# Four edits at the head of a decoder layer's first projection: who asks for the loads, who casts, in what pieces

## The chip, the cores and the metric

The kernel runs on one core of a Trainium2 chip. A core has five engines with instruction rows of their own: TensorE (PE in the profile; PEld is its weight load), VectorE (DVE), ScalarE (ACT), GpSimd (POOL) and SyncE (SP). Any of SP, ScalarE and GpSimd can ask for a load; 16 DMA engines then move it. An engine works its row in order and waits where a semaphore is not there yet. The metric is device time in microseconds, the median over several executions of the same program; one execution is profiled.

## The reference

One layer of a decoder over 272 rows (16 meta tokens and 256 of input) of width 2048. Only the first projection is touched by the change; the rest is given in outline.

```python
u = rmsnorm(h, norm_mix)
proj = u @ w_in            # 2048 x 7176: q, k, v, gates of 8 retention and 4 mLSTM heads
...
ret = head_norm(retention_chunkwise(...)) * silu(g_r)
hm = head_norm(mlstm_chunkwise(...)) * sigmoid(o_m)
h = h + concatenate([ret, hm]) @ w_out
u = rmsnorm(h, norm_ffn)
up = causal_dwconv(u @ w_up, ffn_conv_w, ffn_conv_b)
gate, val = split(up)
h = h + (silu(gate) * val) @ w_down
out = rmsnorm(h, norm_final)[N_META:]
```

## The kernel before

**Number format.** Every product is made in three matmuls. A float32 operand is split into a high part (a cast to float32r) and a low part (the rest), and high x high, high x low and low x high are summed in PSUM. For weights, the cast is on ScalarE (`whi`) and the subtraction on VectorE (`wlo`); for the activations likewise (`xh` on ScalarE, scaled by the norm's weight; `xl` on VectorE). The scale by the row's root mean square comes after the product, so no matmul has to wait for the norm.

**The ramp** (lines 206 to 238) is the start of the program. The contraction over 2048 is cut into 16 k tiles of 128. The loop takes k = 0 and k = 1 alone and then seven pairs. For each step it loads `hT` (the transposed input, 272 columns for a k tile) and `wraw` (320 columns of weights for a k tile: 128 for a key, 128 for a query, 64 for the gates, from `in_w0`), makes `xh`, `xl`, `whi`, `wlo`, and a low part of the gate weights (line 227, written behind the high part in `whi`), and issues eight matmuls for a k tile: three for the key (`k_ps`), three for the query (`q_ps`), two for the gates (`gates_ps`, lines 235, 236 and 238). Lines 130, 131 and 133 are the three matmuls of the helper `mmk`. `par` holds all small parameters; its first 16 columns are the norm's weights, which every `xh` and `xl` reads.

**Who asks for the loads.** The weights of k = 0 and of k = 1 are asked for by ScalarE, all else by SP, in the order of the loop. `wraw` has four buffers, so the fifth load waits until VectorE is done with the first. The first `xT` load, `par`'s first columns and the rest of the `xT` loads stand on SP one behind another.

**Warm-up.** Before the loop TensorE runs `WARM` matmuls of `ones` with itself, whose result is not used; they start when VectorE has set `ones` (line 171), its third memset.

**Behind the ramp** come 108 loads of 512 KB for the rest of the projection (`load_w`: cast on ScalarE, line 121; low part on VectorE, line 123), the first of them for `v0_ps`, the sum of squares for the norm (line 252 squares, line 255 adds), and then the heads, the output projection, the up-projection and the down-projection, all in the same style. A scheduler sets the final order of each engine's row from the order and the priorities in the code.

Of the kernel before, what the change touches and what calls it, by code (L numbers as in the profile page):

```python
# [10 lines left out]
F32 = mybir.dt.float32  # L11
F32R = mybir.dt.float32r
AF = mybir.ActivationFunctionType
ALU = mybir.AluOpType
PSUM = bass.MemoryType.PSUM

P = 128
# [14 lines left out]
HALF = KT // 2  # L32
GW = 64
W0 = GW + 2 * P
WARM = 8

# [45 lines left out]
def trunk(ctx: ExitStack, tc: tile.TileContext, io, out: bass.AP):  # L84
# [19 lines left out]
        return par[:, a + i : a + i + n]  # L104

    inv_dm = consts.tile([P, P], F32, name="inv_dm")
    nc.vector.memset(inv_dm, 1.0 / DM)
    epsc = consts.tile([P, 1], F32, name="epsc")
    nc.vector.memset(epsc, EPS)
    rstd2 = consts.tile([P, NQ], F32, name="rstd2")  # L110


# [56 lines left out]
    ident = pa.tile([P, P], F32, name="ident")  # L169
    ones = pa.tile([P, P], F32, name="ones")  # L170
    nc.vector.memset(ones, 1.0)
    inv_ret = pa.tile([P, P], F32R, name="inv_ret")
    inv_ml = pa.tile([P, P], F32R, name="inv_ml")
    rstd1 = pa.tile([P, T], F32, name="rstd1")
# [10 lines left out]
    kpad = [pa.tile([P, 3 * P], F32, name=f"kpad{i}") for i in range(2)]  # L185
    vpad = pa.tile([P, 3, 2 * P], F32, name="vpad")
    ppad = pa.tile([P, ABC], F32, name="ppad")
    for kt in kpad:
        nc.gpsimd.memset(kt[:, T:], 0.0)
    nc.gpsimd.memset(vpad[:, 2, :], 0.0)  # L190
# [15 lines left out]
    with pool("sq", 1, side="right") as sqp:  # L206
        for k0, k1 in [(0, 1), (1, 2)] + [(k, k + 2) for k in range(2, KT, 2)]:
            n = k1 - k0
            nc.sync.dma_start(hT[:, k0:k1, :], io["xT"][:, k0:k1, :])
            if k0 == 0:  # L210
                nc.sync.dma_start(par[:, 0:KT], io["par"][:, 0:KT])
            raw = wpool.tile([P, 2, W0], F32, name="wraw", bufs=4)[:, :n, :]

            queue = nc.scalar if k0 < 2 else nc.sync
            load = queue.dma_start(raw, io["w0"][:, k0:k1, :])
            if k0 >= 2:
                last_load = load
            for k in range(k0, k1):
                nc.scalar.activation(xh[:, k, :], hT[:, k, :], AF.Copy, scale=pcol("gmix", k))
                nc.vector.scalar_tensor_tensor(out=xl[:, k, :], in0=hT[:, k, :], scalar=pcol("gmix", k),  # L220
                                               in1=xh[:, k, :].bitcast(F32), op0=ALU.mult, op1=ALU.subtract)

            hi = wpool.tile([P, 2, W0 + GW], F32R, name="whi", bufs=5)[:, :n, :]
            copied = nc.scalar.copy(hi[:, :, 0:W0], raw)
            lo = wpool.tile([P, 2, 2 * P], F32R, name="wlo", bufs=5)[:, :n, :]
            nc.vector.tensor_tensor(out=lo, in0=raw[:, :, 0 : 2 * P], in1=hi[:, :, 0 : 2 * P].bitcast(F32), op=ALU.subtract)
            parted = nc.vector.tensor_tensor(out=hi[:, :, W0:], in0=raw[:, :, 2 * P :], in1=hi[:, :, 2 * P : W0].bitcast(F32), op=ALU.subtract)
            for k in range(k0, k1):
                i = k - k0
                first, last = k == 0, k == KT - 1  # L230
                for j, (ps, t0) in enumerate(((k_ps, 0), (q_ps, TQ))):
                    w = hi[:, :, j * P : (j + 1) * P], lo[:, :, j * P : (j + 1) * P]
                    mmk(ps[:, : T - t0], w, [(i, k)], lambda k: xh[:, k, t0:], lambda k: xl[:, k, t0:], 0, KT - 1)
                if not last:
                    nc.tensor.matmul(gates_ps[:, :T], hi[:, i, 2 * P :], xh[:, k, :], start=first, stop=False)
                nc.tensor.matmul(gates_ps[0:GW, :T], hi[:, i, 2 * P : W0], xl[:, k, :], start=False, stop=False)
                if last:
                    nc.tensor.matmul(gates_ps[:, :T], hi[:, i, 2 * P :], xh[:, k, :], start=False, stop=True)
# [830 lines left out]
```

## Time and profile before

| what | us |
|---|---|
| runs shown | 1208.54, 1208.73, 1211.33 |
| their median | 1208.73 |
| the profiled execution | 1207.7 |
| its span, first to last instruction | 1205.9 |
| TensorE busy in the span | 1194.6 |
| ScalarE, VectorE, GpSimd busy | 709.5, 971.5, 162.8 |

The span is shorter than the execution's own time by what lies around the program's instructions (1.8 us). Busy time of TensorE counts matmuls with their modelled ends, so matmuls that follow one another overlap in it. Times in the timeline are counted from the start of the span.

### The profile page before, as it was taken

How to read it: one execution, taken by the hardware profiler on the slowest of the kernel's cores; microseconds unless marked ns; L12 is line 12 of the kernel's file. 1: busy time of each engine (PE TensorE's matmuls, PEld its weight loads, DVE VectorE, ACT ScalarE, POOL GpSimd, SP SyncE). 2: the span in 40 equal slices, each digit the busy share in tenths (PEclk: the TensorE clock that was granted, in tenths of full speed). 3: DMA queues.
4: the chain of work that ended last, by engine and by line, in shares of the span. 5: the costliest groups of instructions: out<-in, count | busy, mean ns of one | idle time of the engine just before them, and what ended most of it. 6: DMA issues, size and time to landing. Idle time of an engine off the chain costs nothing.

```text
span 1205.9 us, 22794 instructions
## 1 busy us (share of the span) xinstructions
PE 1194.6 (99%) x8956; PEld 1151.2 (95%) x8956; DVE 971.5 (81%) x1444; ACT 709.5 (59%) x963; POOL 162.8 (14%) x223
## 2 busy tenths in 40 slices
PE   9999999999999999999999999999999999999997
PEld 9999999999999999999999998878999999998886
DVE  8968788766775966789889879897788778789897
ACT  8747656655656646555555557664555555556664
POOL 0100001111110311021122100202022112100232
PEclk9999999999999999999999999999999999999999
DMA  8765555666565965766766834959787777755956
GB/s 278 269 212 164 170 184 170 197 183 192 169 192 165 349 200 175 252 220 212 253 219 214 279 117 175 278 177 276 284 251 255 223 240 249 261 176 211 274 181 186
DMA packets 83004, 263.27 MB, mean 218 GB/s; under 512 B 14672, under 2 KB 18896, under 8 KB 82768
## 3 DMA queue, kind: packets, MB, share of 16 engines
q1 hardware_dynamic: 71952, 223.85, 57.0%
q0 software_dynamic: 10368, 37.11, 10.1%
q8 instruction: 70, 1.15, 0.4%
q10 hardware_dynamic: 576, 0.85, 0.2%
q14 instruction: 38, 0.31, 0.1%
HBM read 243.42 MB, written 11.27 MB: 211 GB/s over the span
## 4 chain that ended last, share of the span: by engine, by line
PE 96%; DMA 2%; DVE 1%; ACT 0%; issue 0%; SPq 0%; DVEq 0%; ACTq 0%
PE mmps L130 26%; PE mmps L131 25%; PE mmps L133 25%; PE atps L827 2%; PE atps L828 2%; PE atps L830 2%; PE mmps L860 2%; PE mmps L862 2%; PE mmps L859 2%; PE atps L862 1%; PE atps L860 1%; PE atps L859 1%; DMA hn<-x 1%; PE atps L379 1%; DMA hT<-in_wd 1%; PE atps L371 0%
## 5 line engine op out<-in xcount | busy, mean ns | idle before, releaser
L121 ACT CAST whi<-wraw 128x1024 fp32r<-128x1024 f32 x352 | 369.3, 1050 | 342.0 <-PE mmps L131 228.7
L123 DVE TENSOR_TENSOR wlo<-wraw,whi 128x1024 fp32r<-128x1024 f32 x352 | 432.3, 1230 | 72.5 <-ACT whi L121 70.0
L130 PE MATMUL mmps<-uh,whi 128*128 128x258 f32 x1408 | 346.1, 283 | 0.0
L131 PE MATMUL mmps<-ul,whi 128*128 128x258 f32 x1408 | 346.0, 283 | 0.0
L130 PEld LDWEIGHTS mmps<-uh,whi 128*128 128x128 f32 x1408 | 267.6, 190 | 0.1
L131 PEld LDWEIGHTS mmps<-ul,whi 128*128 128x128 f32 x1408 | 267.1, 190 | 0.1
L130 PE MATMUL mmps<-xh,whi 128*128 128x272 f32 (+2 forms) x864 | 219.8, 288 | 0.0
L131 PE MATMUL mmps<-xl,whi 128*128 128x272 f32 (+2 forms) x864 | 218.3, 286 | 0.0
L133 PE MATMUL mmps<-uh,wlo 128*128 128x258 f32 x1408 | 196.5, 282 | 0.0
L133 PEld LDWEIGHTS mmps<-uh,wlo 128*128 128x128 f32 x1408 | 179.9, 189 | 0.0
L131 PEld LDWEIGHTS mmps<-xl,whi 128*128 128x128 f32 x864 | 162.8, 188 | 0.0
L130 PEld LDWEIGHTS mmps<-xh,whi 128*128 128x128 f32 x864 | 162.5, 188 | 0.1
L133 PE MATMUL mmps<-xh,wlo 128*128 128x272 f32 (+2 forms) x864 | 126.7, 285 | 0.0
L133 PEld LDWEIGHTS mmps<-xh,wlo 128*128 128x128 f32 x864 | 114.2, 188 | 0.0
L680 DVE TENSOR_TENSOR cu<-mmps,rstd 128x258 f32<-128x258 f32 x88 | 37.4, 425 | 55.3 <-PE mmps L133 54.8
L764 ACT CAST whi<-hT 128x1024 fp32r<-128x1024 f32 x52 | 53.6, 1052 | 27.2 <-PE atps L828 7.3
L766 DVE TENSOR_TENSOR wlo<-hT,whi 128x1024 fp32r<-128x1024 f32 x52 | 62.1, 1220 | 4.9 <-ACT whi L764 3.7
L131 PE MATMUL mmps<-mixl,whi 128*128 128x258 f32 x256 | 63.0, 283 | 0.0
L130 PE MATMUL mmps<-mixh,whi 128*128 128x258 f32 x256 | 62.4, 282 | 0.0
L764 ACT CAST whi<-wraw 128x1024 fp32r<-128x1024 f32 (+1 forms) x52 | 43.0, 838 | 16.8 <-PE mmps L860 6.8
L766 DVE TENSOR_TENSOR wlo<-wraw,whi 128x1024 fp32r<-128x1024 f32 (+1 forms) x52 | 52.2, 1037 | 0.6 <-PE mmps L862 0.2
L827 PE MATMUL atps<-whi,mh 128*128 128x512 f32 (+1 forms) x132 | 50.9, 387 | 1.3 <-ACT whi L121 1.1
(280 smaller groups left out, 1700.1 us busy)
## 6 DMA issues: line engine op xcount, KB each, us to landing
wraw<-in_wu SPq DMA_DIRECT2D x176, 512.0 KB, 4.4
wraw<-in_wi SPq DMA_DIRECT2D x108, 512.0 KB, 4.1
hT<-in_wd SPq DMA_DIRECT2D x26, 768.0 KB, 4.7
wraw<-in_wd SPq DMA_DIRECT2D x36, 512.0 KB, 4.7
wraw<-in_wo SPq DMA_DIRECT2D x32, 512.0 KB, 4.2
x<-in_wd POOLq DMA_DIRECT2D x13, 768.0 KB, 7.0
hn<-x POOLq DMA_DIRECT2D x27, 256.0 KB, 7.9
hT<-kept SPq DMA_DIRECT2D x26, 256.0 KB, 2.9
```

The source lines that it names most:

```text
L121: nc.scalar.copy(hi, raw)
L123: nc.vector.tensor_tensor(out=lo, in0=raw, in1=hi.bitcast(F32), op=ALU.subtract)
L130: nc.tensor.matmul(ps, hi[:, k, :], xh(kk), start=kk == first, stop=False)
L131: nc.tensor.matmul(ps, hi[:, k, :], xl(kk), start=False, stop=False)
L133: nc.tensor.matmul(ps, lo[:, k, :], xh(kk), start=False, stop=kk == last)
L680: evacuated = nc.vector.tensor_tensor(out=u, in0=ps[:, :NQ], in1=rstd2, op=ALU.mult)
L764: copied = nc.scalar.copy(hi, x)
L766: return copied, nc.vector.tensor_tensor(out=lo, in0=x, in1=hi.bitcast(F32), op=ALU.subtract)
L827: nc.tensor.matmul(ps, ah[i], hi[:, i, cols], start=first and i == 0, stop=False)
L859: nc.tensor.matmul(o, sh[:, f, m, :], hi[:, i, :], start=begin, stop=False)
L860: nc.tensor.matmul(o, sl[:, f, m, :], hi[:, i, :], start=False, stop=False)
L862: nc.tensor.matmul(o, sh[:, f, m, :], lo[:, i, :], start=False, stop=end)
```

## The change

The change has five edits, all in the ramp or just ahead of it.

1. GpSimd asks for the norm's weights (`par`, 8 KB) as the first thing in its row, ahead of its memsets; SP no longer does.
2. ScalarE asks for the weights of k = 2, 3 as well (its third issue); SP does so from k = 4 on.
3. VectorE makes the high part of the first weight load; ScalarE still makes all others.
4. The weights of k = 2, 3 come in one load as before, but cast, low part and gate part are made for each k tile by itself. `xh` of k = 3 is ordered behind the cast of k = 2's weights, and `xl` moves behind the low part in the code.
5. `ones` is VectorE's first memset instead of its third, and there are seven warm-up matmuls instead of eight.

```diff
--- before.py
+++ after.py
@@ -32,7 +32,7 @@
 HALF = KT // 2
 GW = 64
 W0 = GW + 2 * P
-WARM = 8
+WARM = 7
 
 
 
@@ -104,9 +104,7 @@
         return par[:, a + i : a + i + n]
 
     inv_dm = consts.tile([P, P], F32, name="inv_dm")
-    nc.vector.memset(inv_dm, 1.0 / DM)
     epsc = consts.tile([P, 1], F32, name="epsc")
-    nc.vector.memset(epsc, EPS)
     rstd2 = consts.tile([P, NQ], F32, name="rstd2")
 
 
@@ -169,6 +167,8 @@
     ident = pa.tile([P, P], F32, name="ident")
     ones = pa.tile([P, P], F32, name="ones")
     nc.vector.memset(ones, 1.0)
+    nc.vector.memset(inv_dm, 1.0 / DM)
+    nc.vector.memset(epsc, EPS)
     inv_ret = pa.tile([P, P], F32R, name="inv_ret")
     inv_ml = pa.tile([P, P], F32R, name="inv_ml")
     rstd1 = pa.tile([P, T], F32, name="rstd1")
@@ -185,6 +185,7 @@
     kpad = [pa.tile([P, 3 * P], F32, name=f"kpad{i}") for i in range(2)]
     vpad = pa.tile([P, 3, 2 * P], F32, name="vpad")
     ppad = pa.tile([P, ABC], F32, name="ppad")
+    nc.gpsimd.dma_start(par[:, 0:KT], io["par"][:, 0:KT])
     for kt in kpad:
         nc.gpsimd.memset(kt[:, T:], 0.0)
     nc.gpsimd.memset(vpad[:, 2, :], 0.0)
@@ -207,24 +208,27 @@
         for k0, k1 in [(0, 1), (1, 2)] + [(k, k + 2) for k in range(2, KT, 2)]:
             n = k1 - k0
             nc.sync.dma_start(hT[:, k0:k1, :], io["xT"][:, k0:k1, :])
-            if k0 == 0:
-                nc.sync.dma_start(par[:, 0:KT], io["par"][:, 0:KT])
             raw = wpool.tile([P, 2, W0], F32, name="wraw", bufs=4)[:, :n, :]
 
-            queue = nc.scalar if k0 < 2 else nc.sync
+            queue = nc.scalar if k0 < 4 else nc.sync
             load = queue.dma_start(raw, io["w0"][:, k0:k1, :])
-            if k0 >= 2:
+            if k0 >= 4:
                 last_load = load
-            for k in range(k0, k1):
-                nc.scalar.activation(xh[:, k, :], hT[:, k, :], AF.Copy, scale=pcol("gmix", k))
-                nc.vector.scalar_tensor_tensor(out=xl[:, k, :], in0=hT[:, k, :], scalar=pcol("gmix", k),
-                                               in1=xh[:, k, :].bitcast(F32), op0=ALU.mult, op1=ALU.subtract)
-
             hi = wpool.tile([P, 2, W0 + GW], F32R, name="whi", bufs=5)[:, :n, :]
-            copied = nc.scalar.copy(hi[:, :, 0:W0], raw)
             lo = wpool.tile([P, 2, 2 * P], F32R, name="wlo", bufs=5)[:, :n, :]
-            nc.vector.tensor_tensor(out=lo, in0=raw[:, :, 0 : 2 * P], in1=hi[:, :, 0 : 2 * P].bitcast(F32), op=ALU.subtract)
-            parted = nc.vector.tensor_tensor(out=hi[:, :, W0:], in0=raw[:, :, 2 * P :], in1=hi[:, :, 2 * P : W0].bitcast(F32), op=ALU.subtract)
+            for c0, c1 in [(0, 1), (1, 2)][:n] if k0 < 4 else [(0, 2)]:
+                for k in range(k0 + c0, k0 + c1):
+                    with tc.issue_after(copied.ins) if k == 3 else nullcontext():
+                        nc.scalar.activation(xh[:, k, :], hT[:, k, :], AF.Copy, scale=pcol("gmix", k))
+                if k0 == 0:
+                    nc.vector.tensor_copy(hi[:, c0:c1, 0:W0], raw[:, c0:c1])
+                else:
+                    copied = nc.scalar.copy(hi[:, c0:c1, 0:W0], raw[:, c0:c1])
+                nc.vector.tensor_tensor(out=lo[:, c0:c1], in0=raw[:, c0:c1, 0 : 2 * P], in1=hi[:, c0:c1, 0 : 2 * P].bitcast(F32), op=ALU.subtract)
+                for k in range(k0 + c0, k0 + c1):
+                    nc.vector.scalar_tensor_tensor(out=xl[:, k, :], in0=hT[:, k, :], scalar=pcol("gmix", k),
+                                                   in1=xh[:, k, :].bitcast(F32), op0=ALU.mult, op1=ALU.subtract)
+                parted = nc.vector.tensor_tensor(out=hi[:, c0:c1, W0:], in0=raw[:, c0:c1, 2 * P :], in1=hi[:, c0:c1, 2 * P : W0].bitcast(F32), op=ALU.subtract)
             for k in range(k0, k1):
                 i = k - k0
                 first, last = k == 0, k == KT - 1
```

Line numbers in the rows of the changed program are its own: 222 is the `xh` line, 224 VectorE's new cast, 226 ScalarE's cast, 227 the low part, 229 `xl`, 231 the gate part, 210 and 214 the loads of `hT` and `wraw`.

ScalarE, from the start of the program. Before:

```order
L215 DMA wraw<-in_w 128x320 x2
L224 ACT_TABLE_LOAD
L224 CAST whi<-wraw 128x320
L219 ACTIVATE xh<-hT,par 128x272
L224 CAST whi<-wraw 128x320
L219 ACTIVATE xh<-hT,par 128x272 x3
L224 CAST whi<-wraw 128x2x320
L219 ACTIVATE xh<-hT,par 128x272 x2
```

and of the change:

```order
L214 DMA wraw<-in_w 128x320 x2
L214 DMA wraw<-in_w 128x640
L222 ACT_TABLE_LOAD
L222 ACTIVATE xh<-hT,par 128x272 x2
L226 CAST whi<-wraw 128x320
L222 ACTIVATE xh<-hT,par 128x272
L226 CAST whi<-wraw 128x320
L222 ACTIVATE xh<-hT,par 128x272
L226 CAST whi<-wraw 128x320
```

The first cast has gone, the first two xh stand ahead of any cast, and the pair cast of k = 2, 3 (128x2x320, behind three xh in a row) has become two casts of 128x320, each behind one xh.

VectorE, from its first memset. Before:

```order
L107 MEMSET inv_dm 128x128
L109 MEMSET epsc 128x1
L171 MEMSET ones 128x128
L282 MEMSET hj_451 4x272
L299 MEMSET y 128x258
L226 TENSOR_TENSOR wlo<-wraw,whi 128x256
L227 TENSOR_TENSOR whi<-wraw,whi 128x64
L220 SCALAR_TENSOR_TENSOR xl<-hT,par,xh 128x272
L226 TENSOR_TENSOR wlo<-wraw,whi 128x256
L227 TENSOR_TENSOR whi<-wraw,whi 128x64
L220 SCALAR_TENSOR_TENSOR xl<-hT,par,xh 128x272 x3
```

and of the change:

```order
L169 MEMSET ones 128x128
L170 MEMSET inv_dm 128x128
L171 MEMSET epsc 128x1
L286 MEMSET hj_453 4x272
L303 MEMSET y 128x258
L224 CAST whi<-wraw 128x320
L227 TENSOR_TENSOR wlo<-wraw,whi 128x256
L231 TENSOR_TENSOR whi<-wraw,whi 128x64
L229 SCALAR_TENSOR_TENSOR xl<-hT,par,xh 128x272 x2
L227 TENSOR_TENSOR wlo<-wraw,whi 128x256
L231 TENSOR_TENSOR whi<-wraw,whi 128x64
L229 SCALAR_TENSOR_TENSOR xl<-hT,par,xh 128x272
```

`ones` has moved to the front, the cast of 128x320 stands ahead of the first low part, and the first two `xl` follow the first weights' parts.

SyncE, at the end of the ramp's loads (k = 8 to 15 and then a piece of `par`). Before:

```order
L209 DMA hT<-in_xT 128x544
L215 DMA wraw<-in_w 128x640
L209 DMA hT<-in_xT 128x544 x2
L215 DMA wraw<-in_w 128x640
L209 DMA hT<-in_xT 128x544
L215 DMA wraw<-in_w 128x640 x2
L240 DMA par<-in_par 128x58
```

and of the change:

```order
L210 DMA hT<-in_xT 128x544
L214 DMA wraw<-in_w 128x640
L210 DMA hT<-in_xT 128x544 x3
L214 DMA wraw<-in_w 128x640 x3
L244 DMA par<-in_par 128x58
```

The last load of `hT` (k = 14, 15) now stands ahead of the weights of k = 10, 11 instead of behind them.

## Rows read from the trace of the kernel before

**Rows 1.** The page: busy time, share of the span and instructions of each engine.

```profile
PE 1194.6 (99%) x8956; PEld 1151.2 (95%) x8956; DVE 971.5 (81%) x1444; ACT 709.5 (59%) x963; POOL 162.8 (14%) x223
```

**Rows 2.** The chain that ended last, 0 to 12 us: start, us, what.

```profile
0.74 0.39 SPq L209
...
1.19 0.42 SPq L211
...
2.12 4.15 DMA hT<-in_xT
...
6.29 0.94 ACT xh L219 x2
...
7.24 0.73 ACT whi L224
```

**Rows 3.** Timeline of TensorE: start us, us, operation, count, [idle before <-releaser].

```profile
1.21 3.79 PE L199 MATMUL atps<-ones 128*128 128x128 f32 x16 [1.21 <-DVE ones L171]
...
4.89 0.39 PE L130 MATMUL atps<-xh,whi 128*128 128x272 f32 x1
...
5.47 0.39 PE L131 MATMUL atps<-xl,whi 128*128 128x272 f32 x1
...
7.05 0.29 PE L236 MATMUL atps<-xl,whi 128*64 128x272 f32 x1
...
8.02 0.39 PE L130 MATMUL atps<-xh,whi 128*128 128x272 f32 x1 [0.68 <-ACT whi L224]
...
10.34 0.28 PE L130 MATMUL atps<-xh,whi 128*128 128x272 f32 x1
...
10.84 0.29 PE L133 MATMUL atps<-xh,wlo 128*128 128x272 f32 x1
...
16.25 0.29 PE L130 MATMUL atps<-xh,whi 128*128 128x272 f32 x1
...
24.23 1.17 PE L133 MATMUL atps<-xh,wlo 128*128 128x272 f32 x8
```

**Rows 4.** Timeline of ScalarE in the ramp.

```profile
3.95 0.46 ACT L224 CAST whi<-wraw 128x320 fp32r<-128x320 f32 x1 [1.01 <-DMA wraw<-in_w]
...
8.81 0.71 ACT L224 CAST whi<-wraw 128x640 fp32r<-128x640 f32 x1
...
14.50 0.71 ACT L224 CAST whi<-wraw 128x640 fp32r<-128x640 f32 x1
```

**Rows 5.** Windows: busy time by engine, granted clock, DMA share, GB/s.

```profile
4.00:5.00 1.00, 1.00 (x6) 0.81 (x6) 0.56 (x3) 1.00 (x3) 0.00 (x0) 1.00 0.80 126
...
10.00:12.00 2.00, 2.00 (x19) 2.00 (x17) 1.98 (x6) 2.00 (x5) 0.00 (x0) 1.00 1.03 403
```

**Rows 6.** Timeline of VectorE.

```profile
4.44 0.43 DVE L226 TENSOR_TENSOR wlo<-wraw,whi 128x256 fp32r<-128x256 f32 x1 [2.74 <-ACT whi L224]
...
9.63 0.69 DVE L226 TENSOR_TENSOR wlo<-wraw,whi 128x512 fp32r<-128x512 f32 x1
...
22.78 2.34 DVE L123 TENSOR_TENSOR wlo<-wraw,whi 128x1024 fp32r<-128x1024 f32 x2
...
39.27 0.30 DVE L265 TENSOR_SCALAR rstd<-r 128x272 f32<-128x272 f32 x1
```

**Rows 7.** DMA issues of single stretches, KB, us to landing.

```profile
wraw<-in_w SPq DMA_DIRECT2D x1, 320.0 KB, 4.6
...
hT<-in_xT SPq DMA_DIRECT2D x1, 136.0 KB, 3.0
...
par<-in_par SPq DMA_DIRECT2D x1, 8.0 KB, 2.9
...
e<-in_decay POOLq DMA_DIRECT2D x1, 209.0 KB, 5.2
```

**Rows 8.** The decay table's tile `e`, the whole run: its loads.

```profile
L415 POOL DMA_DIRECT2D e<-in_decay x8: 553/556/731, 125.0 to 345.8; - x8
...
DMA to landing us min/median/max: 2.9/3.2/5.2
```

**Rows 9.** Timeline of SyncE's issues.

```profile
2.60 0.43 SPq L215 DMA_DIRECT2D wraw<-in_w  x1
```

## The prediction

> **What bounds the kernel now.** The page comes first: TensorE is busy for 1194.6 of 1205.9 us [rows 1], so only 11.3 us of the span are not matmul, and only the part of it that lies in the ramp can be touched. Then the chain of work over the first microseconds, which shows what the end of the ramp hangs on: the load of hT for k = 2, 3 lands 4.15 us after 2.12, then two xh, then one cast of both k tiles, then TensorE at 8.02 [rows 2]. TensorE's timeline shows the same place as its one named wait after the warm-ups, 0.68 us for that cast, and gives the dates that must move: warm-ups 1.21 to 5.0, k = 0 from 4.89, the last matmul of k = 1 at 7.05 (so free at 7.17), k = 2 at 8.02, k = 4 at 10.34 with its first low-part matmul at 10.84, k = 10 at 16.25 [rows 3]. From 10.34 to 16.25 lie 48 matmuls, 0.123 us each, 0.985 us for a k, with no idle: from there TensorE is its own limit. So the whole prize is an earlier 8.02 and, a little, an earlier 4.89, provided that what feeds k = 4 to 15 can follow.
>
> What feeds it is DMA: ScalarE's first cast waits for its load until 3.95, and its casts at 8.81 and 14.50 start as their loads land [rows 4]. The DMA engines move 403 GB/s at 10 to 12 us, but only 126 at 4 to 5 [rows 5].
>
> **The change, step by step.** I follow center values; the ends come after.
>
> *First matmul.* It needs xh 0 and the high part of weight 0. Today ScalarE makes both, the cast from 3.95 [rows 4] and then the xh, and the first matmul follows at 4.89 [rows 3]. Afterwards VectorE casts at 3.95. No row has this cast there: the same cast on ScalarE takes 0.46 [rows 4], a VectorE operation with one tensor input from SBUF takes 0.30 for 272 columns [rows 6]; I take 0.35, nearer the second, since it is the same engine: ready at 4.30. xh 0 needs hT 0, issued at 0.74 [rows 2] with 3.0 to landing [rows 7], so 3.74, and par. From SP par was issued at 1.19 and took 2.9 (4.09). From GpSimd it is issued at about 0.74; GpSimd's loads of the decay table took 2.9 to 5.2, median 3.2 [rows 8]; the median gives 3.94, so xh 0, 0.52 long with its end (two take 0.94, [rows 2]), is done at 4.46. The first matmul gains 0.4.
>
> The Trainium skill ("DMA: Bandwidth & Descriptors", section Latency and other measured facts) speaks against this edit: it puts the first byte of a GpSimd load at about 1 us and of an SP load at 0.6. By it par would land at 0.74 + 2.9 + 0.4 = 4.04 and the first matmul 0.1 later than in my sum; the minimum of GpSimd's rows, 2.9, is no longer than SP's 2.9.
>
> *The seven warm-ups* need only `ones`, now VectorE's first memset instead of its third (about 0.15 earlier). Seven eighths of 3.79 us [rows 3] from 1.06 end at 4.38, before 4.46: removing the eighth costs nothing while xh 0 comes before about 4.5. If it comes later, nothing covers that time.
>
> *k = 0 and 1.* xl 0 stands behind the low part and the gate part on VectorE. Before, that row began at 4.44 [rows 6] and TensorE first used xl 0 at 5.47 [rows 3]: 1.03 for the row. Now it begins behind VectorE's own cast, at 4.30: 5.33. Five matmuls follow it: k = 0 ends at 5.95 instead of 6.19, k = 1 at 6.95 instead of 7.17. Half of the first matmul's gain is lost here, because VectorE's row gained less than ScalarE's.
>
> *The gap before k = 2.* Moving par off SP brings every later SP issue 0.47 forward (its 0.42 and the pause, the chain's own piece [rows 2]). hT 2, 3 then lands at 5.80 if its latency is fixed and at 6.27 if bandwidth sets it; I take 6.0. The weights of k = 2, 3 are asked for at about 1.66, behind two other issues on ScalarE from 0.74, instead of at 2.60 [rows 9]; with the same 4.6 us [rows 7] they land at 6.3. ScalarE now needs one xh (0.45) and one cast of 320 columns (0.4) before TensorE can go, instead of 0.94 and 0.73: 6.85. That is before 6.95, so the gap closes and k = 3 ends at 8.95: 1.39 ahead of 10.34. The third issue on ScalarE (0.45) delays its table load, which still ends by 3.4, before hT 0 lands; so it is free.
>
> *k = 4, 5 take some of it back.* Their weights landed just before 8.81. The bytes ahead of them are the same; all that can make them earlier is the hole at 4 to 5 us. The hole leaves 277 KB unmoved, 0.69 us at 403 GB/s, if the earlier weight load fills it all; nothing if the hole stays. I take a third, 8.5. ScalarE is done with two xh by 8.6, the cast takes 0.71 [rows 4], VectorE's low part 0.69 [rows 6]: ready at 10.0. Its first use was at 10.84 [rows 3]. So TensorE is 0.8 ahead, not 1.39.
>
> *k = 10, 11 take more.* On SP the load of hT for k = 14, 15 now goes ahead of the weights of k = 10, 11: 272 KB, again 0.69 us. The cast that starts at 14.50 moves to 14.50 - 0.25 + 0.69 = 14.9; with 0.71 and 0.69 the low part is there at 16.3. Before, it was used half a microsecond after 16.25. The lead shrinks to about **0.5 us**. Loads of k = 12 to 15 have the same bytes ahead as before and are in time.
>
> *Behind the ramp.* The first low part of the next weights is ready at 22.78 + 1.17 = 23.95 and used at 24.23 [rows 3, 6]: 0.28 of slack. ScalarE's casts and squares ahead of it move with the landings, 0.25 or more, and VectorE now makes this low part before the gate copy instead of after it, so a lead of 0.5 passes. Later instructions keep their order but for single rows.
>
> **Sum.** 0.22 (k = 0, 1) + 1.17 (gap and k = 2, 3) - 0.59 (k = 4, 5) - 0.30 (k = 10, 11) = 0.5 us of 1205.9. The profiled execution took 1207.7, so 1207.2 for it; the median of the runs shown lies 1.03 above that execution, and I forecast the median: 1208.73 - 0.5 = **1208.2 us**. Ends of this case: landing times unimproved and par at the slow end of tolerable, -0.1; the hole fully filled, -1.0: 1207.7 to 1208.6.
>
> **Rivals.**
> *Bandwidth keeps it all (no gain).* For: from 6 us on, landings follow bytes, and loads were only reordered. If the hole stays and k = 10's weights come 0.69 later, their low part is there at 16.6, against a use at 16.75: 0.15 left. Time 1208.6; with a first wi low part that does not move either, 1208.7. Against: it needs the hole to stay whole.
>
> *Par comes late (slower).* Every xh stands behind it, and ScalarE's row now begins with two xh. The first of GpSimd's eight decay loads, its first load in the program, is the one at 5.2 [rows 7]. At 5.2 par lands at 5.94, xh 0 is done at 6.46, ScalarE then has five xh, three casts of 320 and one of 640 ahead of the end of k = 4, 5's cast (5 x 0.45 + 3 x 0.38 + 0.71 = 4.1): 10.5, low part at 11.3 against 10.84, so 0.5 us slower: 1209.2. It turns from gain to loss where par lands after 5.4, and each microsecond beyond costs one. To pass 3.6 us, par would need until about 9. The skill's section named above makes this rival likelier than SP's rows alone would, without reaching 5.4 itself.
>
> *The clock.* The granted clock reads 1.00 in the rows here [rows 5], but the first matmuls now follow seven warm-ups and perhaps a pause. If k = 0 and 1 ran at 1.2 instead of 2.4 GHz, five and eight matmuls at 0.246 us from 5.33 end at 8.5, and k = 3 at 10.45: 0.1 slower, 1208.8. If k = 2 and 3 did so too, 2.1 slower, 1210.8. For it: one warm-up less. Against: TensorE has work from about 1.06 on, 0.15 earlier than before.
>
> *More than 1 us.* All landings 0.7 or more earlier and no loss at k = 10: 1207.2.
>
> **Chances.** Forecast 0.55; bandwidth 0.2; par late 0.12; clock 0.06; more than 1 us 0.07. Range: the cases lie between 1207.2 and 1209.2, with 1210.8 at the far end; the three runs shown spread from 1208.54 to 1211.33 and the profiled one is at 1207.7, so the median of a few runs moves by about 0.7 by itself. I take **1206.8 to 1210.0**. A difference under 0.3%, 3.6 us, is about what a measurement of this kernel cannot tell from no change, and all cases above lie within it: faster 0.02 (the ramp has no 3.6 us to give: all idle and warm-up from 3.74 on sums to under 2.1), within 0.95, slower 0.03 (par at 9 us, or low clock beyond k = 3).
>
> **What would show it.** First real matmul at 4.4 to 4.6 and ready for k = 2 at 7 without a named wait; k = 4's first low-part matmul near 10.0; a short wait at k = 10; the matmul now at 24.23 near 23.7. Wrong, if: xh 0 starts after 5 because of par; the wait before k = 2 stays; the low parts of k = 4 or 10 are as late as before; or the matmuls of k = 0 start more than 0.2 us apart back to back.

## The result and the profile after

| kernel | median, us | runs | lowest to highest |
|---|---|---|---|
| before, same comparison | 1208.57 | 22 | 1206.42 to 1211.33 |
| after | 1212.66 | 22 | 1208.43 to 1216.70 |

The ratio is 1.0032, with an interval of 1.0023 to 1.0041: about 4 us slower, where 0.5 us less was forecast, and outside the range. A second comparison gave 1210.64 against 1208.46 us (10 and 12 runs), ratio 1.0025, 1.0014 to 1.0037. The profiled execution of the changed kernel took 1216.7 us (span 1214.9), the slowest of its 22, so three profiles of the change are compared further down.

In the changed program 188 is GpSimd's load of `par`, 222 the `xh`, 224 VectorE's cast, 226 ScalarE's, 227 and 229 `wlo` and `xl`; 128, 129 and 131 are the three matmuls of the helper. TensorE's busy time of the page, against [rows 1]:

```profile
PE 1197.1 (99%) x8954; PEld 1153.1 (95%) x8954; DVE 970.8 (80%) x1447; ACT 705.7 (58%) x963; POOL 171.1 (14%) x224
```

The span grew by 9.0 us and the busy time by 2.5, so 6.5 us of the difference are idle TensorE. The list of TensorE's waits says where (us in total, times, longest; before, the first two causes had 1.1 and 0.2, and the ramp's one named wait, for the cast of k = 2, had 0.7):

```profile
PE atps L831 <- ACT whi L119: 3.3, 4, 1.7
PE atps L831 <- ACT x L955: 2.7, 2, 2.2
PE atps L128 <- ACT xh L222: 2.5, 1, 2.5
```

The last row is the ramp; the first two lie in the down-projection, where no edit is (last experiments). The timeline of TensorE in the ramp, to be laid beside [rows 3]:

```profile
1.06 3.35 PE L200 MATMUL atps<-ones 128*128 128x128 f32 x14 [1.06 <-DVE ones L169]
6.92 0.59 PE L128 MATMUL atps<-xh,whi 128*128 128x272 f32 x1 [2.51 <-ACT xh L222]
...
12.45 0.43 PE L128 MATMUL atps<-xh,whi 128*128 128x272 f32 x1
...
12.84 0.29 PE L129 MATMUL atps<-xl,whi 128*128 128x272 f32 x1
...
13.59 0.29 PE L128 MATMUL atps<-xh,whi 128*128 128x272 f32 x1
...
27.49 1.17 PE L131 MATMUL atps<-xh,wlo 128*128 128x272 f32 x8
```

The first real matmul starts at 6.92 instead of 4.89, after 2.51 us of idle. The starts from 7.31 to 12.45 are 23 steps of 0.223 us for 262 or 272 columns, 1.2 columns a ns, which is TensorE's lower level of 1.2 GHz; behind 12.84 the starts are 0.12 apart, as between 10.34 and 16.25 in [rows 3]. (The granted-clock column of the windows reads 1.00 through all of it; spacing and the length of a row, 0.43 against 0.29, show the level.) k = 4 begins at 13.59 instead of 10.34. The last row is the first low-part group of the weights behind the ramp, at 24.23 in [rows 3]; I use it as the **mark** of what the ramp cost: here 3.26 us. It stays as large through the next 600 us (the 5000th matmul behind the warm-ups, counted in both traces, starts at 622.43 against 619.12).

What held the first matmul is in the chain that ended last,

```profile
0.64 0.65 issue
1.29 5.04 DMA par<-in_par
...
6.35 0.53 ACT xh L222
```

and in ScalarE's timeline:

```profile
0.74 1.38 ACTq L214 DMA_DIRECT2D wraw<-in_w  x3
3.77 1.28 ACT L222 ACT_TABLE_LOAD   x1 [3.77 <-DMA hT<-in_xT]
6.35 0.94 ACT L222 ACTIVATE xh<-hT,par 128x272 fp32r<-128x272 f32 x2 [1.29 <-DMA par<-in_par]
```

Two things stand ahead of `xh` 0. The norm's weights leave GpSimd at 1.29, not 0.74, and land 5.04 us later. And ScalarE's table load, 1.28 us, no longer runs in the idle time before the loads land: it waits for `hT` 0. Before, the first thing that ScalarE computed was a cast with one load to wait for, and the table load ahead of it waited for none:

```profile
1.66 1.28 ACT L224 ACT_TABLE_LOAD   x1 [1.66 <-PEq L1059]
```

Now it is an `xh` with two, and in the program's order the table load ahead of it carries one of the two waits. In this execution that cost nothing, because the table load ended at 5.05 and `par` landed at 6.33. The loads asked for from 0.5 to 1.72 us, KB and us to landing (the 272 KB are `hT` for k = 2, 3, the 320 KB their weights):

```profile
wraw<-in_w ACTq DMA_DIRECT2D x1, 320.0 KB, 6.2
...
hT<-in_xT SPq DMA_DIRECT2D x1, 272.0 KB, 6.0
par<-in_par POOLq DMA_DIRECT2D x1, 8.0 KB, 5.0
```

The hole of [rows 5], 126 GB/s from 4 to 5 us, is filled, and the start is no earlier for it:

```profile
4.00:5.00 1.00, 0.41 (x2) 0.12 (x1) 0.79 (x3) 1.00 (x1) 0.00 (x0) 1.00 1.04 377
```

### The profile page after: what moved, and what is told of

Same layout as the page of the kernel before. It is cut to its first block, busy times and chain, and to the rows that moved or that the text cites. A ratio compares the mean times of both kernels' runs of the same rounds, so it can differ in the third digit from the quotient of the medians.

```text
span 1214.9 us, 22792 instructions
## 1 busy us (share of the span) xinstructions
PE 1197.1 (99%) x8954; PEld 1153.1 (95%) x8954; DVE 970.8 (80%) x1447; ACT 705.7 (58%) x963; POOL 171.1 (14%) x224
## 4 chain that ended last, share of the span: by engine, by line
PE 93%; DMA 4%; DVE 1%; issue 1%; ACT 1%; DVEq 0%; SPq 0%; ACTq 0%; POOLq 0%
PE mmps L128 25%; PE mmps L129 25%; PE mmps L131 25%; PE atps L831 2%; PE atps L832 2%; DMA wraw<-in_wd 2%; PE atps L834 2%; PE mmps L866 1%; PE mmps L864 1%; PE mmps L863 1%; PE atps L864 1%; PE atps L863 1%; PE atps L866 1%; DMA hn<-x 1%; PE atps L383 1%
## 5 line engine op out<-in xcount | busy, mean ns | idle before, releaser
L882 POOL DMA_DIRECT2D hn<-x x27 | 23.6, 1077 | 207.3 <-ACT x L888 173.8
```

## The experiments

The theories: **A**, the norm's weights from GpSimd are late and everything stands behind them; **B**, the scheduler's new order behind the ramp loses the time; **C**, the pause after the warm-ups has TensorE work at its lower level behind it. Later came the held table load, and **D**, VectorE's order inside the ramp. Ratios are to the kernel before, in the same comparison; "mark" is the row at 24.23 of [rows 3] (24.28 and 24.00 in two more profiles of before).

| run | median, us | ratio, interval | first matmul | mark |
|---|---|---|---|---|
| after | 1212.66 | 1.0032, 1.0023 to 1.0041 | 6.92 | 27.49 |
| e11, e12: the change again | 1210.64, (one run) 1211.51 | 1.0025, 1.0014 to 1.0037 | 5.57, 5.49 | 25.51, 25.78 |
| e1: par back on SP | 1212.46 | 1.0037, 1.0023 to 1.0050 | 6.04 | 27.21 |
| e4: 18 warm-ups | 1209.03 | 1.0016, 1.0005 to 1.0027 | 6.83 | 25.62 |
| e6, e14: table loaded early | 1210.61, (one run) 1211.19 | 1.0027, 1.0013 to 1.0041 | 5.24, 6.33 | 25.23, 26.93 |
| e7b, e13: third load back on SP | 1209.86, (one run) 1207.01 | 1.0013, 1.0004 to 1.0022 | 5.47, 5.72 | 25.61, 25.48 |
| e2: before, par on GpSimd | 1209.03 | 1.0007, 0.9997 to 1.0017 | 5.90 | 24.32 |
| e5: before, unused GpSimd load | (one run) 1207.11 | | 4.85 | 23.93 |
| e9: before, the casts alone | 1208.81 | 1.0007, 0.9998 to 1.0016 | 5.87 | 25.33 |
| e9t: the same, table early | 1208.67 | 1.0004, 0.9995 to 1.0013 | 4.65 | 24.81 |
| e15: the same, VectorE's old order | 1207.99 | 0.9999, 0.9989 to 1.0009 | 4.72 | 24.18 |

**e1, the change with the norm's weights asked for by SP again.**

```diff
-    nc.gpsimd.dma_start(par[:, 0:KT], io["par"][:, 0:KT])
...
+            if k0 == 0:
+                nc.sync.dma_start(par[:, 0:KT], io["par"][:, 0:KT])
```

> The change with the norm's weights asked for by SP again, as its second issue. Theory A (GpSimd's first load is late, and all else of the loss follows from it): the first xh no longer waits for par; it starts behind ScalarE's table load, which now waits for hT 0 (3.75 to 5.05), so at about 5.05, and the first matmul at about 5.6 instead of 6.92. If the pause of 1.2 us behind the seven warm-ups leaves the clock alone, the marker (first low-part matmul of v0_ps, 24.23 before and 27.49 - 3.02 or later in the change) comes within 0.5 us of 24.23 and the median within 1 us of before. If the pause alone costs the clock, matmuls are 0.22 us apart for some microseconds and the time stays 1 to 2.5 us above before. Rival B (the loss is in the reordered casts and loads, not in par): the marker stays 2 us or more behind although par is in time.

The weights were in time, and nothing was won. ScalarE's timeline shows the table load holding up the `xh`, behind the landing of `par` this time,

```profile
4.17 1.28 ACT L223 ACT_TABLE_LOAD   x1 [4.17 <-DMA par<-in_par]
5.46 0.52 ACT L223 ACTIVATE xh<-hT,par 128x272 fp32r<-128x272 f32 x1
```

and VectorE's shows an effect that the edit itself brought in: the scheduler put the copy of the gates, which needs the end of the ramp's matmuls, ahead of the sums and of the low part behind the ramp (`wlo`), so that TensorE waited 1.74 us there:

```profile
23.50 0.43 DVE L289 COPY g<-atps 4x272 f32<-4x272 f32 x1 [3.14 <-PE atps L243]
...
25.95 2.34 DVE L121 TENSOR_TENSOR wlo<-wraw,whi 128x1024 fp32r<-128x1024 f32 x2
```

The change's own order doesn't have this, so B is not what the change costs, and e1 can't be read by its time.

**e2, the kernel before with only the norm's weights moved to GpSimd; e5, before with an unused 8 KB load from GpSimd.** The edit of e2 is the reverse of e1's, made in the kernel before; e5 adds

```diff
+    spare = pa.tile([P, KT], F32, name="spare")
+    nc.gpsimd.dma_start(spare, io["par"][:, 0:KT])
```

> The kernel before with one edit: the norm's weights asked for by GpSimd. Theory A: par lands at about 6.3, the first xh starts there, the first matmul at 6.9 after eight warm-ups that end at 5.0; the clock is low for several microseconds after it; the marker comes 2 to 3.3 us after 24.23 and the median is 2 to 4 us above before. Rival B: par in this place costs under 0.5 us, since xh has other things to wait for.

> The kernel before with one load added: GpSimd asks for the same 8 KB into a tile that nothing reads, first in its row; par itself stays on SP. If a first GpSimd load of the program is late for being the first: the spare load takes about 5 us from issue to landing, and the first load of the decay table at 125 us, then the second GpSimd load, takes about 3.2 instead of 5.2. If it is late for the moment (saturated DMA engines at the start): the decay load stays at 5.2. Time as before within 1 us either way, since nothing reads the tile.

In e2 ScalarE's first work is a cast, so its table load is done early (1.66), and `par`, issued at 1.28, lands 4.0 us later:

```profile
1.66 1.28 ACT L223 ACT_TABLE_LOAD   x1 [1.66 <-PEq L1058]
...
5.32 0.94 ACT L218 ACTIVATE xh<-hT,par 128x272 fp32r<-128x272 f32 x2 [1.05 <-DMA par<-in_par]
```

The first matmul is 1.0 us late, yet the mark, 24.32, moves by 0.09: what lies ahead of k = 2 takes it up. A alone, with `par` at 5.3, is not enough; a landing at 6.3, as in the first profile, was not seen with this edit alone. In e5 the load is again issued at 1.28 and took 3.2 us, and the first load of the decay table, now GpSimd's second, took 4.6 where it took 5.2 as the first [rows 7]; being the first is not what delays such a load:

```profile
spare<-in_par POOLq DMA_DIRECT2D x1, 8.0 KB, 3.2
```

**e4, the change with 18 warm-up matmuls.**

```diff
-WARM = 7
+WARM = 18
```

> The change with 18 warm-up matmuls instead of 7. Theory C (the low clock is a cost of its own, brought by the 2.5 us without matmuls): the warm-ups run until 6.2 to 6.6, the first real matmul stays at about 6.9 because of par, matmuls are then 0.123 us apart from the start, k = 4 begins near 11 and the marker is 0.5 to 1.2 us behind 24.23 instead of about 3.3; median 0.5 to 1.5 us above before. Rival (the clock rises at its own date whatever runs ahead, or the loss is the feeding of k = 0 to 5): matmuls of k = 0 to 3 still 0.22 us apart, the marker 3 us behind or more.

The weights were as late as in the first profile (5.0 us to landing), but TensorE had no pause:

```profile
1.06 5.86 PE L200 MATMUL atps<-ones 128*128 128x128 f32 x36 [1.06 <-DVE ones L169]
6.83 0.39 PE L128 MATMUL atps<-xh,whi 128*128 128x272 f32 x1
...
25.62 1.16 PE L131 MATMUL atps<-xh,wlo 128*128 128x272 f32 x8
```

With nearly the same start the mark is 1.87 us earlier (27.49 - 25.62): by these two profiles that is what the lower level cost, and 1.39 of the 3.26 us remain for the rest. The time follows in part: the ratio is 1.0016 in place of 1.0032 and 1.0025, with intervals that overlap.

**e7b and e13, the change with the third weight load on SP again** (the order of every other engine is the change's):

```diff
-            queue = nc.scalar if k0 < 4 else nc.sync
+            queue = nc.scalar if k0 < 2 else nc.sync
...
-            if k0 >= 4:
+            if k0 >= 2:
```

**e6 and e14, the change with the table loaded ahead of everything,** one line ahead of the warm-ups:

```diff
+    nc.scalar.preload_act_table_set("natural_log_exp_and_others")
```

> The change with only the third weight load asked for by SP again; every engine's instructions are otherwise in the change's order, so whatever differs comes from that load. Theory A (crowded queues: the norm's weights need 5.0 us from issue to landing because a third load stands in ScalarE's queue beside SP's): issue at 1.28, landing about 4.0 us later as in the run with GpSimd alone moved, first real matmul near 5.9 instead of 6.92, the low clock ends earlier by about as much, v part at 23.3 instead of 25.5, time about 1210.4. Theory B (a GpSimd load is slow by itself in this kernel, whoever else asks): landing 5.0 us after the issue, first real matmul near 6.9, time about 1212.6 as the change.

> The change with the third weight load on SP, a second look. If that load is what makes the norm's weights late, they land about 3.6 us after the issue as in its first look and first real matmul is near 5.5; if the landing is chance, it falls anywhere from 3.4 to 5.0 us after the issue, as in the two looks at the change.

> The change with ScalarE's activation table loaded ahead of everything it computes, so that the load no longer waits for hT 0. Theory A (the norm's weights set the start; the table load, 3.77 to 5.05, lies beside their wait): the first xh still begins near 6.35, first real matmul near 6.9, time as the change, about 1212.6. Theory C (the held table load is what costs): the first xh begins 1.28 earlier, first real matmul near 5.6, v part at 23.3 or earlier, time about 1210.

> The change with the table loaded early, a second look (its first had the norm's weights 3.4 us after the issue and no low clock, though its 12 times reached from 1207.2 to 1214.6). If the third load makes them late, this look has them at 5.0 us, first real matmul near 6.9 and the low clock to about 12.7; if the early table load itself helps them, 3.4 us and 5.2 as before.

`par`'s time to landing does not simply follow the third load: 3.4 and 3.8 us without it on ScalarE's queue, but 5.0, 3.5, 3.4 in three profiles of the change, 5.0 in e4, 3.4 and 4.5 in e6 and e14. It scatters by 1.6 us between executions of one and the same order. The three landings above 4.0 us all have the third load on ScalarE; whether that load makes them likelier (crowded queues, my reading of the first profile) ten profiles don't settle. What does follow the third load is the load of `hT` for k = 2, 3. The same stretch of e7b, KB and us to landing:

```profile
hT<-in_xT SPq DMA_DIRECT2D x1, 272.0 KB, 4.5
par<-in_par POOLq DMA_DIRECT2D x1, 8.0 KB, 3.4
```

It took 4.5 and 4.1 us here and in e13, and 5.0 to 7.2 in the six executions with the load on ScalarE and `par` on GpSimd (6.0, 5.0, 5.8, 5.9, 5.6, 7.2). And the weights themselves, asked for some 0.9 us sooner than at 2.60, took 5.9 to 7.4 us in place of 4.6 [rows 7]. In e1, with that load on ScalarE but `par` on SP and the weights of k = 4, 5 asked for at 3.79 instead of 2.60, both took 4.7. This fits the bytes asked for by about 2.6 us: 1192 KB in the order of before (`hT` of k = 2, 3 in 3.9 to 4.4 us, in seven profiles), 1464 KB in e1, e2, e7b and e13 (4.1 to 4.7), 1784 KB in the change's order (5.0 to 7.2). No run moves the bytes and nothing else, so this is a reading that fits, not one that is shown. In e12, where nothing else hides it, this is ScalarE's timeline at k = 2:

```profile
3.62 1.28 ACT L222 ACT_TABLE_LOAD   x1 [3.62 <-DMA hT<-in_xT]
...
7.51 0.52 ACT L222 ACTIVATE xh<-hT,par 128x272 fp32r<-128x272 f32 x1 [1.31 <-DMA hT<-in_xT]
8.21 0.46 ACT L226 CAST whi<-wraw 128x320 fp32r<-128x320 f32 x1 [0.18 <-DMA wraw<-in_w]
```

The cast of k = 2 alone starts at 8.21, behind the 7.24 of the cast for both k tiles in [rows 2]. In e7b and e13 these casts start at 7.01 and 7.09, but TensorE is at its lower level until about 10.3 and 9.8, after pauses of 1.06 and 1.31 us, and the marks are no better than the change's.

In e6 the early table let `xh` 0 start at 4.66, when `par` landed, and the mark still came out at 25.23, 1.0 late; in e14 `par` landed at 5.8 and the mark was 2.70 late. The time of e6, 1.0027, is that of the change. So no run shows that the change's time hangs on the held table load: with the table early, late `par`, the loads of k = 2, 3, VectorE's order and the lower level still cost 1.0 and 2.7 us in the ramp.

The times say one thing that the profiles don't. Of the change, e4, e6, e11, e12 and e14, which have the third load on ScalarE and `par` on GpSimd, 24 of 57 executions took more than 1212 us; of all kernels with that load on SP, the kernel before included, none of some 170 did (highest 1211.52, in e7b). e7b differs from the change by that load alone, and in its own comparison e6 had 5 of 12 above, e7b none of 12. The long executions were thus seen only with the third load on ScalarE; how they become long is open, since only one of them, the change's first, was profiled.

**e11 and e12, the changed kernel again, unedited.**

> The changed kernel again, unedited, to see how much of its trace repeats. Theory A (its ramp is what costs): the norm's weights issued at 1.28 and landed well past 5, first real matmul 6 to 7, the low clock after it, and matmul number 1000 at 133 to 134 (before 130.8); time about 1212. Rival (its first profile was a rare one): landing near 4.6, first real matmul near 6.0, matmul 1000 near 132, time about 1210. The down-projection, 5 us longer in the first profile than before, is expected to come out 1 to 3 us longer here, because it varied by 3.5 us among the eight other profiles without an edit near it.

> The changed kernel a third time, one look. The same numbers as for the run before it; if the landing of the norm's weights is set by the queues alone it repeats within 0.3 us between the two, if it is chance it spreads from 3.4 to 5.0 us after the issue.

The first profile was an extreme one, as e11's rival had it. TensorE in e11,

```profile
5.57 0.60 PE L128 MATMUL atps<-xh,whi 128*128 128x272 f32 x1 [1.16 <-ACT xh L222]
...
9.54 0.43 PE L129 MATMUL atps<-xl,whi 128*128 128x272 f32 x1
...
10.14 0.29 PE L131 MATMUL atps<-xh,wlo 128*128 128x272 f32 x1
...
25.51 1.17 PE L131 MATMUL atps<-xh,wlo 128*128 128x272 f32 x8
```

and in e12:

```profile
5.49 0.39 PE L128 MATMUL atps<-xh,whi 128*128 128x272 f32 x1 [1.07 <-ACT xh L222]
...
8.72 0.40 PE L128 MATMUL atps<-xh,whi 128*128 128x272 f32 x1 [0.82 <-ACT whi L226]
...
18.22 0.39 PE L131 MATMUL atps<-xh,wlo 128*128 128x272 f32 x1 [0.37 <-DVE wlo L227]
...
25.78 1.17 PE L131 MATMUL atps<-xh,wlo 128*128 128x272 f32 x8
```

The same program, the same start within 0.1 us, the same pause of 1.1 us: once at the lower level until about 10, once not at all. But the one at the higher level lost as much, 1.55 against 1.28: it waited 0.82 at k = 2 and 0.37 at k = 10. So C is real in its cost, 1.9 us where the start was latest, but the pause is not seen to lower the clock: the change's 14 warm-up rows, after the first, start 0.21 to 0.22 us apart to their end, and e4's do so until about 4.4 us, from where they start 0.11 apart. TensorE had not left its lower level when the seven warm-ups ended; what follows the pause is a late rise, near 12.7 in the first profile and 10.0 in e11, while in e12 it came before 5.49. There another cost took its place. The two can also meet: e14 is at the lower level until 10.05, waits 0.33 at k = 10, and has its mark at 26.93. The shorter pauses of e6 (0.83 us) and e2 (0.91) were followed by no lower level, that of e9 (1.03) was, although e9 has eight warm-ups; no run gives the change its eighth warm-up back, so what that alone is worth is not measured.

**e9, e9t and e15: the casts alone, in the kernel before.** Queues and the eight warm-ups are those of before. e9 has VectorE's cast, the split casts, the place of `xl` behind the low part and the early memset of `ones` of the change, its core being

```diff
-            copied = nc.scalar.copy(hi[:, :, 0:W0], raw)
...
+                if k0 == 0:
+                    nc.vector.tensor_copy(hi[:, c0:c1, 0:W0], raw[:, c0:c1])
+                else:
+                    copied = nc.scalar.copy(hi[:, c0:c1, 0:W0], raw[:, c0:c1])
```

and the loop over the two k tiles around it; e9t adds the early table load as above; e15 adds to e9t

```diff
+                if k0 == 10:
+                    low10 = low
...
+                    with tc.issue_after(low10.ins) if k0 == 14 else nullcontext():
```

around the `xl` (`low` is the `wlo` instruction), so that the `xl` of k = 14, 15 stand behind the low part of k = 10, 11, as before the change.

> The kernel before with VectorE's cast of the first weights and the one by one casts of k = 0 to 3 alone; both queues and the 8 warm-up matmuls are as before. The first computing instruction of ScalarE is now xh, with two loads to wait for, so if a held table load is a cost of its own, it shows here: table load at about 4.1, first real matmul near 6.0, a pause of about 1.0 us after the warm-ups, and since that pause was absorbed in the run with GpSimd alone moved, v part near 22.3 and the time within 0.3% of before, about 1208.7. If the table load is not held, first real matmul near 4.6 and v part at or before 22.2, about 1208.0.

> The same with the table loaded early: queues and warm-ups as before, casts as in the change. Expected by every theory: the first xh right after hT 0 and the norm's weights, near 4.1, first real matmul 4.6 (before 4.89), no pause worth naming after the warm-ups, no matmul at the low clock. If the gap before k = 2 is set by loads, as the run with GpSimd alone moved suggests, most of that is given back there and the v part starts near 22.0, time 1208.0 to 1208.6; if it is set by ScalarE's casts (the prediction's reading), the one by one casts shorten it and the v part starts near 21.0, time about 1207.3.

> The kernel with the change's casts, the queues and warm-ups of before and the table loaded early, now with VectorE's last two xl put behind the low part of k = 10 and 11, as in the order of before; nothing else moves on VectorE. Theory D (the order is what loses the time there): no wait of TensorE at 16.6 to 17.3, the step from k = 10 to k = 12 back from 2.58 to 1.97, v part at 22.2 or earlier instead of 22.80, matmul 1000 at 130.8 or earlier, time 1207.5 to 1208.5. Rival (VectorE is full there whatever its order, since it casts the first weights too): v part still near 22.8 and the wait moved to k = 14.

In e9 the table load waits until 4.00 (for `par`, from SP), the first matmul comes at 5.87, the matmuls are at the lower level until 9.2, and the mark is 1.10 late, where the pause was expected to be taken up:

```profile
4.00 1.28 ACT L223 ACT_TABLE_LOAD   x1 [4.00 <-DMA par<-in_par]
```

```profile
5.87 0.60 PE L128 MATMUL atps<-xh,whi 128*128 128x272 f32 x1 [1.03 <-ACT xh L223]
...
25.33 1.17 PE L131 MATMUL atps<-xh,wlo 128*128 128x272 f32 x8
```

With the table early, e9t starts at 4.65, 0.24 before the kernel before, with no pause; its mark is still 0.58 late, and TensorE's timeline says why:

```profile
4.65 0.50 PE L128 MATMUL atps<-xh,whi 128*128 128x272 f32 x1
...
17.25 0.39 PE L131 MATMUL atps<-xh,wlo 128*128 128x272 f32 x1 [0.34 <-DVE wlo L229]
...
24.81 1.17 PE L131 MATMUL atps<-xh,wlo 128*128 128x272 f32 x8
```

It waits for the low part of k = 10, 11. VectorE in e9t,

```profile
14.04 2.56 DVE L231 SCALAR_TENSOR_TENSOR xl<-hT,par,xh 128x272 fp32r<-128x272 f32 x6
16.52 0.68 DVE L229 TENSOR_TENSOR wlo<-wraw,whi 128x512 fp32r<-128x512 f32 x1
```

and in e15:

```profile
13.91 1.74 DVE L234 SCALAR_TENSOR_TENSOR xl<-hT,par,xh 128x272 fp32r<-128x272 f32 x4
15.86 0.69 DVE L229 TENSOR_TENSOR wlo<-wraw,whi 128x512 fp32r<-128x512 f32 x1 [0.21 <-ACT whi L228]
```

Six `xl` stand ahead of that low part in the change's order, four in that of before:

```profile
13.80 1.73 DVE L220 SCALAR_TENSOR_TENSOR xl<-hT,par,xh 128x272 fp32r<-128x272 f32 x4
15.45 0.69 DVE L226 TENSOR_TENSOR wlo<-wraw,whi 128x512 fp32r<-128x512 f32 x1
```

With the order put back, the wait is gone and the mark is at 24.18. D is shown in the traces, at 0.63 us; the times, 1.0004 and 0.9999, are too close to show it. And e15 is the best that these edits gave: 0.9999 of before, so none of the kernels tried is shown to beat it. It starts 0.17 earlier, k = 4 begins 0.48 earlier (9.86 against 10.34), and by the mark 0.05 is left. Most of this goes between k = 4 and k = 6 (12.17 against 12.32), where TensorE's first low-part matmul follows the low part's end at 10.53; VectorE's timeline has no idle time from 7.6 to 15.6, so VectorE holds it there.

**e18 and e19, the kernel before again, for the down-projection.**

> The kernel before, one more look, for the spread of its down-projection. If the longer down-projection of the change is chance, the stretch from matmul 5000 to 7000 (294.5 us in the first look) spreads here too, by 1 us or more; if it belongs to the change, it stays within 0.5 us of 294.5. Ramp: matmul 1000 at 130.8 within 0.3.

> The kernel before, a third look, with the same two readings as the look before it: the stretch from matmul 5000 to 7000 spreads by 1 us or more if the down-projection varies by chance, and stays within 0.5 us of 294.5 if not; matmul 1000 at 130.8 within 0.3.

Of 760 to 840 us TensorE was busy 78.89 us in the first profile of before, 78.64 in e18 and 80.00 in e19, and 74.55, 78.01 and 77.60 in the three of the change. From the 5000th to the 7000th matmul, counted in the traces, it took 294.5, 294.9 and 293.0 us before, and 299.7, 295.7 and 296.4 in the change. The row of e19 and then that of the change's first profile:

```profile
760.00:840.00 80.00, 80.00 (x393) 67.28 (x392) 68.14 (x71) 48.57 (x56) 14.03 (x16) 1.00 0.81 240
```

```profile
760.00:840.00 80.00, 74.55 (x324) 59.56 (x323) 68.19 (x71) 43.64 (x50) 10.53 (x12) 1.00 0.75 225
```

So before spreads by 1.9 us as well, and e2 and e15, which cost nothing in the ramp, stand at 77.78 and 77.98 there, like the change; the change's e4 and e13 at 80.00. Most of this looks like chance of the execution. That the change makes the bad cases likelier is possible (its three are the lowest of the six of these two kernels), and is not settled: over all profiles the stretch from 5000 to 7000 takes 292.7 to 296.2 us with the third load on SP, and 292.7 to 299.7 with it on ScalarE, only the change's first lying above 296.4.

## Why the prediction was wrong, step by step

**"The third issue on ScalarE (0.45) delays its table load, which still ends by 3.4, before hT 0 lands; so it is free": this step failed.** It placed the table load by when ScalarE is free, not by what the table load waits for. Moving the first cast to VectorE made an `xh` ScalarE's first work, and the table load took over a wait of that: it ran from 3.6 to 3.8 on, ended at 4.9 to 5.05, and so `xh` 0 was done at 5.4 at best in the three profiles, not at 4.46, and the first real matmul came at 6.92, 5.57 and 5.49 instead of 4.4 to 4.6. That the table load can do this is shown by e9 against e9t: first matmul 5.87 and 4.65, mark 25.33 and 24.81, with no other difference but the early load. In the change it is one of two: `par` landed at 6.33, 4.78 and 4.68, so beside it the held table load cost nothing in the first profile and 0.2 us of the start in e11 and e12, and e6 won no time without it. The Trainium skill ("ScalarE: Activation LUTs", section What ACT_TABLE_LOAD costs) gives some 1283 ns for it, and the trace agrees with 1.28 us.

**The norm's weights: two terms were mis-sized.** The issue is at 1.28, not 0.74, in every kernel whose GpSimd row begins with this load, and the landing takes 3.2 to 5.0 us, not 3.2. No row of before shows a load issued by GpSimd at the start. The Trainium skill's section cited in the prediction ("DMA: Bandwidth & Descriptors", Latency and other measured facts) has the right sign: an estimate from its two first-byte figures is 0.4 us more for the path through GpSimd. The runs show more, 0.55 at the issue alone, and a spread that SP's load of the same bytes doesn't have (2.8 to 2.9 in eight profiles). Alone, in ScalarE's old order, it cost nothing that could be measured (e2: `par` at 5.3, mark 0.09 late), which agrees with the turning point near 5.4 of the rival "par comes late". It bound the start in the first profile; in e11 and e12 the table load did, by 0.2 us.

**"Removing the eighth costs nothing while xh 0 comes before about 4.5. If it comes later, nothing covers that time": right as a condition, and the condition failed.** The seven ended at 4.41 (4.38 forecast). The clock rival, at 0.06, was a mechanism of the first profile and of e11: the sign by which the prediction would know itself wrong, matmuls of k = 0 more than 0.2 us apart, is there. The rival had the whole ramp 2.1 us late with k = 0 to 3 at the lower level; in the first profile it was 3.26 late, of which e4 puts 1.87 on the level. It was held unlikely because TensorE has work 0.15 us earlier; the granted clock that it names reads 1.00 at either spacing and could not have told. By the Trainium skill ("TensorE: Matmul & The Clock Gate", Part 1) how many matmuls run at the lower level differs between runs of one kernel; e11 and e12 agree, and so do the profiles of before: the first seven matmuls were at the lower level in e18 and at the higher in [rows 3].

**"The gap before k = 2 closes": failed, +1.17 in the sum.** The sum gave the weights of k = 2, 3 a fixed 4.6 us from an earlier issue. Asked for sooner, they landed later: cast at 7.75 and 8.21 in e11 and e12, against 7.24 in [rows 2] and 6.85 forecast for its end; and `hT` for k = 2, 3, forecast at 6.0, let `xh` start at 6.71 and 7.51. TensorE's wait at k = 2 was 0.82 in e12, against 0.68 before; in the first profile and in e11 the lower level hid it. The landings fit the bytes asked for in this stretch, which is near the rival "bandwidth keeps it all", though that rival needed the hole to stay and the hole was filled. The step to k = 4, 5 (-0.59) had nothing left to take from: k = 4 began at 13.59, 11.63 and 10.95, not ahead of 10.34. By the times this early load is the step that counts most: taking it back alone gave 1.0013 and no execution above 1212 us (e7b), though the two profiled ramps of that kernel were no shorter.

**k = 10, 11: right place, other cause, size off.** 0.30 was taken for later weights. The loss is VectorE's order, and it is 0.63 (e9t against e15); ScalarE's cast of those weights follows its six `xh` without a wait for the load in e9t and in e12.

**What held:** VectorE's cast (0.35 taken, 0.33 measured, at 3.90), the hole filled, no loss behind the ramp (from the first matmul of the v part to the mark 2.01 us in both, 22.22 to 24.23 and 25.48 to 27.49). In the three profiles the ramp lost 3.26, 1.28 and 1.55 us in place of a gain of 0.5, while their spans were 9.0, 2.9 and 3.8 us longer than that of the first profile of before; 5.2, 1.3 and 1.9 us of this lie between the 5000th and the 7000th matmul. So the ramp is less than half of it in these executions, and the rest lies where the last experiments leave it open. The medians lost 4.1 and 2.2 us.

## What to carry to other kernels

When an instruction is taken off the head of an engine's row, ask what the next one waits for: setup that ran for free in front of the old head (a table load) may now run behind the new one's loads. A load asked for earlier beside others of the same stretch is not earlier by that much; add the bytes ahead of the ones needed first. Before giving away a warm-up, look in several executions whether what follows it is there in time. A gain at the start of a chain is worth what the fullest engine behind it can keep up with, and a row moved by the scheduler there can take it all. One profile of each kernel would have told another story here: the change's first was the slowest of its 22.

## What was not expected of the hardware

A load that opens GpSimd's row starts at 1.28 us where its memset before started at 0.74, and such a load of 8 KB took 3.2 to 5.0 us to land in ten profiles, without a cause found. The same pause of 1.1 us after the warm-ups was followed by 4.4 us of matmuls at the lower level in e11, and by none in e12. The windows' granted clock showed neither.
